# Attention scores in a two-layer decoder kernel: one fp32 product per head, or three products of high and low parts

## The chip, the cores and the metric

The kernel runs on one core of a Trainium2 chip. The metric is the device time of one execution in microseconds, lower is better. TensorE multiplies matrices into PSUM; VectorE, ScalarE and GpSimd work on tiles; SyncE issues the DMAs. Every engine takes its own instructions in the order in which they stand in its list, and waits on semaphores for the others.

## The reference

A causal decoder trunk of two layers on 512 tokens of width 1024, conditioned by a vector. Layer 0 mixes with attention, layer 1 with a state-space layer and a gated delta rule; each is followed by a convolutional feed-forward part. The change lies in layer 0's attention. It has 16 heads of 64 channels in two groups: A (8 query heads on 2 key heads, a window of 128 keys, a learned sink per head) and B (8 heads, three dilated branches). For each head:

```python
qa = rms_norm(qa.reshape(b, L, A_KV_HEADS, rep, HEAD_DIM), q_norm_a)
ka = rms_norm(ka.reshape(b, L, A_KV_HEADS, HEAD_DIM), k_norm_a)
...
s = jnp.einsum("bnqkrd,bnskd->bnkrqs", qb, kw,
               preferred_element_type=jnp.float32) * (hd ** -0.5)
...
s = jnp.where(valid[None, :, None, None], s + bias, -jnp.inf)
m = jnp.max(s, axis=-1, keepdims=True)
p = jnp.exp(s - m)
l = jnp.sum(p, axis=-1)
o = jnp.einsum("bnkrqs,bnskd->bnqkrd", p.astype(v.dtype), vw,
               preferred_element_type=jnp.float32)
```

All of it is float32.

## The kernel before, in words

**Products.** Projections, feed-forward layers and output projections are split products: each operand is held as a high part `hi` (float32 rounded to the type fp32r) and a low part `lo` (what is left), and a product is three, hi x hi, hi x lo and lo x hi, summed in one PSUM bank (`mm3`, lines 392 to 394). Attention's own products are plain fp32: scores (line 806), transposes (760 and 829) and probabilities times values (841).

**Attention** (`attention`, from line 732 on) works in chunks of 256 projected columns. Chunk 0 gives A's keys and values, chunks 1 and 2 A's queries, chunks 3 and 4 B's values, chunks 5 to 8 each one pair of B's heads, queries and keys. `project` multiplies a chunk: two groups of two token blocks, each block 24 products of 256 columns into a bank `acc`. `chunk_post` then normalises (`rmsn`) and calls `to_T`: four transposes on TensorE into bank `t` or `x`, in turn, and one pass on ScalarE (line 763) that scales them and writes an fp32 tile of 128x512, `qT` (four slots) or `kT` (two), or `kTa` for A. The two heads of a pair lie on partitions 0 to 63 and 64 to 127.

`attend` takes a pair through four blocks of 128 queries. `scores` multiplies each head's block of queries by the keys that it sees: in A 128 keys in the first block and 256 in the others, in B 128, 256, 384 and 512. Each head writes one of two banks `s`. Per head there follow on VectorE the bias and row minimum (line 819), on ScalarE the exponentials and their sum (820), on VectorE the reciprocal and the scaling (821 and 822). `values`, one block later, transposes the probabilities into the banks `t` and `x` (829), copies them to `PT` on ScalarE (832) and multiplies them by V into bank `o` (841). After its seventh step `attend` issues one row of the modulation after each block: a DMA and a reduction on VectorE (line 465). When all heads are done, their outputs are split (line 414) and the first output projection (`out_gemm`) begins, which ends attention's stage.

**Order.** A scheduler places instructions by priority and its own estimate of times; `together` keeps a list of products close behind its first one. So the order on each engine is seen in listings of the built program only. The projections of the next chunk, and at the end pieces of the output projection, fill the places between the steps of attention.

The tag of a tile names its slots: tiles of one tag share them in turn. The tags `st`, `whi` and `wlo` in attention's pool `tp` hold one 512 KB weight tile of the first chunks, its high part and its low part, one slot each, and stand empty after these.

Of the kernel before, what the change touches and what calls it, by code (L numbers as in the profile page):

```python
# [8 lines left out]
F32 = mybir.dt.float32  # L9
F32R = mybir.dt.float32r  # L10
I32 = mybir.dt.int32
AF = mybir.ActivationFunctionType
ALU = mybir.AluOpType
# [3 lines left out]
P = 128  # L17
T = 512
# [231 lines left out]
class Kernel:  # L250
# [466 lines left out]
    def attention(self):  # L717
        nc, tc = self.nc, self.tc
        I = self.I
        hA = self.open("hA", "right")  # L720
        tp = self.open("at")
        if True:
# [15 lines left out]
            def rmsn(srcs, n):  # L738

                v = tp.tile([P, 16], F32, name="qv", tag="qv", bufs=2)[:, :4 * n]  # L740
                out = []
                for b, src in enumerate(srcs):
                    qn = tp.tile([P, 2, 256], F32, name="qn", tag="qn", bufs=3)[:, :, :64 * n]
                    nc.scalar.copy(qn, src)
                    out.append(qn)
                for b, qn in enumerate(out):
                    sq = tp.tile([P, 2, 256], F32, name="qsq", tag="qsq", bufs=1)[:, :, :64 * n]
                    nc.scalar.activation(sq, qn, AF.Square)
                    nc.vector.tensor_reduce(v[:, 2 * n * b:2 * n * (b + 1)], sq.rearrange("p t (h d) -> p t h d", d=64), axis=AX.X, op=ALU.add)
                nc.vector.tensor_scalar(v, v, 1.0 / 64.0, EPS, op0=ALU.mult, op1=ALU.add)  # L750
                r = self.rsqrt(tp, v, 4 * n, f"qr{n}")
                for b, qn in enumerate(out):
                    rb = r[:, 2 * n * b:2 * n * (b + 1)].rearrange("p (t h) -> p t h", t=2).unsqueeze(3).broadcast_to([P, 2, n, 64])
                    q4 = qn.rearrange("p t (h d) -> p t h d", d=64)
                    nc.vector.tensor_tensor(q4, q4, rb, ALU.mult)
                return out

            def to_T(qns, g, gain, tag, bufs):
                pt = self.tbank()
                self.together([lambda q=q: nc.tensor.transpose(pt[:, q * P:(q + 1) * P], qns[q // 2][:, q % 2, g * P:(g + 1) * P], self.ident)  # L760
                               for q in range(4)])
                r = tp.tile([P, T], F32, name=tag, tag=tag, bufs=bufs)
                nc.scalar.activation(r, pt, AF.Copy, scale=gain)
                return r

            def chunk_post(c, accs):
                if c == 0:
                    for b in range(2):
                        nc.scalar.copy(V[:, 2 * b:2 * b + 2, 0:128], accs[b][:, :, 128:256])
                    qn = rmsn([a[:, :, 0:128] for a in accs], 2)  # L770
                    self.kTa = to_T(qn, 0, self.pcol("kga"), "kTa", 1)
                elif c in (3, 4):
                    for b in range(2):
                        o = 128 + 256 * (c - 3)
                        nc.scalar.copy(V[:, 2 * b:2 * b + 2, o:o + 256], accs[b])
                else:
                    qn = rmsn(accs, 4)
                    if c in (1, 2):
                        return [to_T(qn, g, self.qg[:, 0:1], "qT", 4) for g in range(2)]
                    return [to_T(qn, 0, self.qg[:, 1:2], "qT", 4), to_T(qn, 1, self.pcol("kgb"), "kT", 2)]  # L780

            def project(c):
                w = [self.weight(("q", c, p)) for p in range(2)]
                return chunk_post(c, [proj(c, b, w) for b in range(2)])
# [3 lines left out]
            def modulation():  # L788

                for g in (*range(16, 20), *range(8, 16)):  # L790
                    for e in range(2):
                        self.ada(0, g, (e,))
                        if e:
                            self.ada_fin(0, g, g + 1, g // 8)
                        yield

            self.step, rows = 0, modulation()

            def scores(pair, i, qT, kT, bias, isA):

                j0 = max(0, i - 1) if isA else 0
                nb = i - j0 + 1
                ps = []
                sbs = [self.bank("s")[:, :nb * P] for _ in range(2)]
                half = [slice(0, 64), slice(64, P)]
                self.together([lambda sb=sb, pr=pr: nc.tensor.matmul(sb, qT[pr, i * P:(i + 1) * P], kT[pr, j0 * P:(i + 1) * P], start=True, stop=True)  # L806
                               for sb, pr in zip(sbs, half)])
                for par, sb in enumerate(sbs):
                    bt = bias[par]
                    bt = bt[:, bt.shape[1] - nb * P:]  # L810
                    S = tp.tile([P, T], F32, name="S", tag="S", bufs=5)
                    E = S[:, :nb * P]
                    if isA:

                        E = S[:, :nb * P + 1]
                        nc.gpsimd.tensor_copy(S[:, nb * P:nb * P + 1], self.nsink[:, 2 * pair + par:2 * pair + par + 1])
                    S = S[:, :nb * P]
                    sm = tp.tile([P, 4], F32, name="sm", tag="sm", bufs=6)
                    nc.vector.tensor_tensor_reduce(S, sb, bt, -1.0, self.nsink[:, 2 * pair + par:2 * pair + par + 1] if isA else 3.0e38, op0=ALU.add, op1=ALU.min, accum_out=sm[:, 0:1])
                    nc.scalar.activation(E, E, AF.Exp, bias=sm[:, 0:1], scale=-1.0, accum_out=sm[:, 1:2])  # L820
                    nc.vector.reciprocal(sm[:, 3:4], sm[:, 1:2])
                    self.last = nc.vector.tensor_scalar(S, S, sm[:, 3:4], None, op0=ALU.mult)
                    ps.append(S)
                return pair, i, j0, nb, ps, isA
# [27 lines left out]
            def attend(pair, qT, kT, isA):  # L852
                bias = []
                for par in range(2):
                    n = 256 if isA else T
                    bt = tp.tile([P, T], F32, name="bt", tag="bt", bufs=3)[:, :n]
                    nc.sync.dma_start(bt, I["ba"][2 * pair + par] if isA else I["bb"][2 * pair + par])
                    bias.append(bt)
                for i in range(4):
                    late.append(scores(pair, i, qT, kT, bias, isA))  # L860
                    self.step += 1
                    if self.step > HELD:
                        with tc.issue_after(self.last.ins):
                            next(rows, None)
                    if len(late) > 1:
                        values(*late.pop(0))
# [57 lines left out]
            for k in range(KD):  # L924
# [9 lines left out]
                for c in range(3):  # L934
# [11 lines left out]
                    if c == 0 and k + 1 in ADA_PE:  # L946
                        next(first[k + 1])
            r = lambda a: a.rearrange("p (t n) -> p t n", t=2)
            chunk_post(0, [r(a) for a in accs[0]])
            qT = dict(zip((0, 1), chunk_post(1, [r(a) for a in accs[1]])))  # L950
            qT.update(zip((2, 3), chunk_post(2, [r(a) for a in accs[2]])))
            attend(0, qT[0], self.kTa, True)
# [4 lines left out]
            qk = project(5)  # L957
            attend(3, qT[3], self.kTa, True)
            for j in range(4):
                nxt = project(6 + j) if j < 3 else None  # L960
                attend(j, *qk, False)
                qk = nxt
# [734 lines left out]
```

## Time and profile before

| | |
|---|---|
| median of 3 runs | 1287.4 us (1284.49 to 1288.83) |
| profiled execution | 1285.57 us, span of its instructions 1283.8 us |
| TensorE busy | 1262.4 us, 98% of the span |
| VectorE busy | 1007.7 us, 78% |
| ScalarE busy | 632.2 us, 49% |
| TensorE clock granted | full in all 40 slices |

The span runs from the first to the last instruction of the profiled execution. PE stands for TensorE's products, PEld for its weight loads, DVE for VectorE, ACT for ScalarE, POOL for GpSimd. Busy times count a product until its result has left the array, so products that follow each other overlap in them. An fp32 product appears as two rows, an fp32r product as one; the profile writes f32 for both types in a product's form. In the chain of work that ended last, each piece is the time for which that work alone held the end back.

### The profile page before, as it was taken

To read this page: it belongs to the slowest core of one execution; us is meant where nothing else is said; L and a number is where in the kernel's file an instruction comes from. 1 tells how busy PE (TensorE), PEld (TensorE's weight loads), DVE (VectorE), ACT (ScalarE), POOL (GpSimd) and SP (SyncE) were. 2 spreads that over 40 slices of the span, in tenths; PEclk is the share of its full clock that TensorE was granted. 3 is DMA by queue.
4 is the path that set the end of the run, shared out by engine and by line. 5 is a ranking of instruction groups with operands and counts; after the bars stand their busy time and mean duration, and the time that the engine had idled before them with its cause. 6 is when DMAs were issued, how large, how long until landed. Compare 5 with 4: busy or idle time off the path is not lost.

```text
span 1283.8 us, 22712 instructions
## 1 busy us (share of the span) xinstructions
PE 1262.4 (98%) x8814; PEld 1079.6 (84%) x8814; DVE 1007.7 (78%) x2195; ACT 632.2 (49%) x1214; POOL 12.3 (1%) x43
## 2 busy tenths in 40 slices
PE   8999999999999999999999999999999999999998
PEld 5988775998888888778998878887999899999998
DVE  6868887679995897587678686775799999888883
ACT  4466655445532332234356555554466555555550
POOL 0001000000000000000000000000000000000000
PEclk9999999999999999999999999999999999999999
DMA  9624444615665676364444332220522223233222
GB/s 368 232 88 153 162 164 159 200 57 196 215 198 192 212 245 207 114 207 160 140 147 134 105 103 64 100 49 35 172 75 99 91 103 104 103 106 108 89 85 103
DMA packets 83133, 181.14 MB, mean 141 GB/s; under 512 B 28561, under 2 KB 36177, under 8 KB 83025
## 3 DMA queue, kind: packets, MB, share of 16 engines
q1 hardware_dynamic: 83024, 179.69, 41.5%
q8 instruction: 69, 1.13, 0.4%
q14 instruction: 40, 0.32, 0.1%
HBM read 165.55 MB, written 14.11 MB: 140 GB/s over the span
## 4 chain that ended last, share of the span: by engine, by line
PE 83%; DVE 9%; DMA 3%; ACT 3%; issue 1%; SPq 0%; DVEq 0%; ACTq 0%
PE acc L393 20%; PE acc L394 10%; PE s L393 10%; PE o L393 9%; PE s L394 5%; PE o L394 5%; PE s L626 3%; PE o L626 2%; PE acc L626 2%; PE s L806 2%; PE o L841 2%; PE x L393 1%; DVE wlo L332 1%; DMA st<-up 1%; DVE adaj L465 1%
## 5 line engine op out<-in xcount | busy, mean ns | idle before, releaser
L363 ACT CAST whi<-st 128x1024 fp32r<-128x1024 f32 (+3 forms) x168 | 165.0, 986 | 223.4 <-PE acc L393 66.3
L364 DVE TENSOR_TENSOR wlo<-st,whi 128x1024 fp32r<-128x1024 f32 (+3 forms) x168 | 191.2, 1140 | 47.2 <-ACT whi L363 45.0
L393 PE MATMUL acc<-hh,whi 128*128 128x512 f32 (+1 forms) x392 | 141.8, 367 | 2.2 <-ACT hh L550 1.8
L393 PE MATMUL acc<-hl,whi 128*128 128x512 f32 (+1 forms) x392 | 141.0, 363 | 0.2 <-DVE hl L414 0.2
L394 PE MATMUL acc<-hh,wlo 128*128 128x512 f32 (+1 forms) x392 | 140.3, 361 | 0.0
L465 DVE CUSTOM_DVE_ANT_0 adaj<-ast,cond 128x1024 bf16<-128x1024 f32 x86 | 104.8, 1219 | 7.3 <-DMA ast<-ada 7.1
L393 PE MATMUL acc<-whi,hh 128*128 128x256 f32 x320 | 93.2, 292 | 0.6 <-ACT hh L550 0.6
L394 PE MATMUL acc<-whi,hl 128*128 128x256 f32 x320 | 90.7, 283 | 0.9 <-DVE hl L551 0.9
L393 PE MATMUL acc<-wlo,hh 128*128 128x256 f32 x320 | 90.6, 284 | 0.0
L393 PE MATMUL s<-hh,whi 128*128 128x512 f32 (+2 forms) x256 | 86.8, 342 | 0.0
L393 PE MATMUL s<-hl,whi 128*128 128x512 f32 (+2 forms) x256 | 86.4, 338 | 0.0
L393 PEld LDWEIGHTS acc<-hh,whi 128*128 128x128 f32 x392 | 73.0, 188 | 15.1 <-ACT hh L550 2.4
L394 PE MATMUL s<-hh,wlo 128*128 128x512 f32 (+2 forms) x256 | 84.6, 338 | 0.0
L393 PEld LDWEIGHTS acc<-hl,whi 128*128 128x128 f32 x392 | 73.4, 188 | 12.1 <-DVE hl L414 1.0
L394 PEld LDWEIGHTS acc<-hh,wlo 128*128 128x128 f32 x392 | 73.4, 188 | 10.8
L331 ACT CAST whi<-st 128x1024 fp32r<-128x1024 f32 x54 | 56.3, 1049 | 28.0 <-DVE st L340 7.8
L393 PE MATMUL o<-hh,whi 128*128 128x512 f32 (+1 forms) x192 | 68.8, 358 | 0.0
L332 DVE TENSOR_TENSOR wlo<-st,whi 128x1024 fp32r<-128x1024 f32 x54 | 65.6, 1217 | 3.8 <-ACT whi L331 3.7
L393 PE MATMUL o<-hl,whi 128*128 128x512 f32 (+1 forms) x192 | 68.6, 357 | 0.0
L394 PE MATMUL o<-hh,wlo 128*128 128x512 f32 (+1 forms) x192 | 68.4, 356 | 0.0
L393 PEld LDWEIGHTS acc<-whi,hh 128*128 128x128 f32 x320 | 60.3, 189 | 6.1 <-issue 4.0
L393 PEld LDWEIGHTS acc<-wlo,hh 128*128 128x128 f32 x320 | 60.5, 189 | 1.6 <-issue 1.6
(909 smaller groups left out, 3468.3 us busy)
## 6 DMA issues: line engine op xcount, KB each, us to landing
ast<-ada SPq DMA_DIRECT2D x92, 512.0 KB
st<-up SPq DMA_DIRECT2D x88, 512.0 KB
st<-ri SPq DMA_DIRECT2D x20, 512.0 KB
st<-wq SPq DMA_DIRECT2D x17, 512.0 KB
st<-dn SPq DMA_DIRECT2D x16, 448.0 KB
st<-dn SPq DMA_DIRECT2D x16, 384.0 KB
st<-dn SPq DMA_DIRECT2D x16, 320.0 KB
st<-wo SPq DMA_DIRECT2D x8, 512.0 KB
```

The costliest lines, as they stand in the source:

```text
L331: nc.scalar.copy(hi, src)
L332: nc.vector.tensor_tensor(lo, src, hi.bitcast(F32), ALU.subtract)
L363: nc.scalar.copy(hi, st)
L364: nc.vector.tensor_tensor(lo, st, hi.bitcast(F32), ALU.subtract)
L393: return [lambda: mm(out, lh, rh, start=start, stop=False), lambda: mm(out, lh, rl, start=False, stop=False), lambda: mm(out, ll, rh, star ...
L394: lambda: mm(out, ll, rh, start=False, stop=stop)]
L465: self.nc.vector.tensor_tensor_reduce(junk, st, self.cond, 1.0, 0.0, op0=ALU.mult, op1=ALU.add, accum_out=self.md[l][:, i:i + 1])
L626: nc.tensor.matmul(acc, x[:, s], y, start=start and k == n == 0, stop=k == 3 and n == 2, skip_group_check=not start)
L806: self.together([lambda sb=sb, pr=pr: nc.tensor.matmul(sb, qT[pr, i * P:(i + 1) * P], kT[pr, j0 * P:(i + 1) * P], start=True, stop=True) f ...
L841: calls.append(lambda j=j, par=par, vc=vc: nc.tensor.matmul(ob[64 * par:64 * par + 64, i * P:(i + 1) * P], V[:, j0 + j, vc:vc + 64], pts[: ...
```

## The change

Queries and keys are split as well. `to_T` still transposes on TensorE; ScalarE now writes the high part, and a new instruction on VectorE computes the low part from the same bank. Both lie in one tile `qk` of 128x2x512 in fp32r. A query tile takes in turn the slots of `st`, `whi`, `wlo` and `qT`; the key tiles, A's too, share the two slots of `kT`. `scores` issues six products per block: hi x hi, hi x lo and lo x hi, each for the one head and then for the other, summed in the two banks `s`. The product lo x lo is left out.

```diff
-            def to_T(qns, g, gain, tag, bufs):
+            def to_T(qns, g, gain, tag):
+
                 pt = self.tbank()
                 self.together([lambda q=q: nc.tensor.transpose(pt[:, q * P:(q + 1) * P], qns[q // 2][:, q % 2, g * P:(g + 1) * P], self.ident)
                                for q in range(4)])
-                r = tp.tile([P, T], F32, name=tag, tag=tag, bufs=bufs)
-                nc.scalar.activation(r, pt, AF.Copy, scale=gain)
-                return r
+                if tag == "qT":
+
+                    tag = ("st", "whi", "wlo", "qT")[self.qturn % 4]
+                    self.qturn += 1
+                t = tp.tile([P, 2, T], F32R, name="qk", tag=tag, bufs=2 if tag == "kT" else 1)
+                hi, lo = t[:, 0], t[:, 1]
+                nc.scalar.activation(hi, pt, AF.Copy, scale=gain)
+                nc.vector.scalar_tensor_tensor(lo, pt, gain, hi.bitcast(F32), ALU.mult, ALU.subtract)
+                return hi, lo
...
-                    self.kTa = to_T(qn, 0, self.pcol("kga"), "kTa", 1)
+                    self.kTa = to_T(qn, 0, self.pcol("kga"), "kT")
...
-                self.together([lambda sb=sb, pr=pr: nc.tensor.matmul(sb, qT[pr, i * P:(i + 1) * P], kT[pr, j0 * P:(i + 1) * P], start=True, stop=True)
-                               for sb, pr in zip(sbs, half)])
+
+                self.together([lambda sb=sb, pr=pr, n=n, a=a, b=b: nc.tensor.matmul(
+                    sb, qT[a][pr, i * P:(i + 1) * P], kT[b][pr, j0 * P:(i + 1) * P], start=n == 0, stop=n == 2)
+                               for n, (a, b) in enumerate(((0, 0), (0, 1), (1, 0))) for sb, pr in zip(sbs, half)])
```

The calls of `to_T` lose their last argument, and `self.qturn` starts at 0.

The scheduler places the stage anew. TensorE, around the transposes of chunk 7's queries and keys (L760 before, L761 now); L806 and L814 are score products, L829 and L838 transposes of probabilities, L393 and L394 products of the projection. Before:

```order
L760 MATMUL t_2138<-ident_71,qn_2112 128x128 x2
L760 MATMUL t_2138<-ident_71,qn_2114 128x128 x2
L760 MATMUL x_2145<-ident_71,qn_2112 128x128 x2
L760 MATMUL x_2145<-ident_71,qn_2114 128x128 x2
L806 MATMUL s_2231<-kT_1857,qT_1850 128x384
L829 MATMUL t_2179<-ident_71,S_1968 128x128 x4
L829 MATMUL x_2180<-ident_71,S_1974 128x128 x4
L393 MATMUL acc_2364<-whi_2003,hh0_163 128x256
```

The change, at the same place:

```order
L761 MATMUL t_2227<-ident_71,qn_2201 128x128 x2
L761 MATMUL t_2227<-ident_71,qn_2203 128x128 x2
L761 MATMUL x_2235<-ident_71,qn_2201 128x128 x2
L761 MATMUL x_2235<-ident_71,qn_2203 128x128 x2
L814 MATMUL s_2330<-qk_1929,qk_1921 128x384 x3
L393 MATMUL acc_2471<-whi_2092,hh0_163 128x256
L393 MATMUL acc_2471<-wlo_2093,hh0_163 128x256
L394 MATMUL acc_2471<-whi_2092,hl0_164 128x256
```

The 24 products of a projection block, of which the last three rows are the first, now stand ahead of the transposes of the probabilities. The score product there is one head's, three rows in line; the other head's come later in both listings.

TensorE, the last block of the last pair, 512 keys, before:

```order
L806 MATMUL s_2718<-kT_2452,qT_2445 128x512
L841 MATMUL o_2680<-PT_2705,V_126 64x128 x2
L806 MATMUL s_2719<-kT_2452,qT_2445 128x512
L841 MATMUL o_2680<-PT_2705,V_126 64x128 x2
L829 MATMUL t_2735<-ident_71,S_2687 128x128 x3
```

The change:

```order
L814 MATMUL s_2855<-qk_2560,qk_2552 128x512
L814 MATMUL s_2856<-qk_2560,qk_2552 128x512
L814 MATMUL s_2855<-qk_2560,qk_2552 128x512
L814 MATMUL s_2856<-qk_2560,qk_2552 128x512
L814 MATMUL s_2855<-qk_2560,qk_2552 128x512
L814 MATMUL s_2856<-qk_2560,qk_2552 128x512
L838 MATMUL t_2876<-ident_71,S_2824 128x128 x3
```

The two heads, apart before, alternate here. Over the whole stage there are 41 runs of score products before and 44 now.

VectorE, the low parts of chunk 8 (L770), in the change; L828, L830 and L831 are the softmax steps of lines 819, 821 and 822 before, L465 a row of the modulation:

```order
L831 TENSOR_SCALAR S_2581<-S_2581,sm_2582 128x128
L465 ISA adaj_2589,md0_75<-ast_2587,cond_72 128x1024
L465 ISA md0_75 128x1
L770 SCALAR_TENSOR_TENSOR qk_2552<-t_2547,qg_127,qk_2552 128x512
L770 SCALAR_TENSOR_TENSOR qk_2560<-x_2555,pc_70,qk_2560 128x512
L478 TENSOR_TENSOR mb0_77<-md0_75,pc_70 128x2
L830 RECIPROCAL sm_2624<-sm_2624 128x1
L828 ISA S_2629,sm_2630<-s_2616,bt_2565 128x256
```

The two low parts stand behind a modulation row and ahead of the next softmax steps.

## Rows read from the trace of the kernel before

**Rows 1.** The page: engines' busy time, and the chain that ended last by engine and line.

```profile
PE 1262.4 (98%) x8814; PEld 1079.6 (84%) x8814; DVE 1007.7 (78%) x2195; ACT 632.2 (49%) x1214; POOL 12.3 (1%) x43
...
PE 83%; DVE 9%; DMA 3%; ACT 3%; issue 1%; SPq 0%; DVEq 0%; ACTq 0%
PE acc L393 20%; PE acc L394 10%; PE s L393 10%; PE o L393 9%; PE s L394 5%; PE o L394 5%; PE s L626 3%; PE o L626 2%; PE acc L626 2%; PE s L806 2%; PE o L841 2%; PE x L393 1%; DVE wlo L332 1%; DMA st<-up 1%; DVE adaj L465 1%
```

**Rows 2.** Busy time of each engine in attention, and in its last 39 us.

```profile
core 0: us, PE busy (x) PEld busy (x) DVE busy (x) ACT busy (x) POOL busy (x), PEclk, DMA share, GB/s
77.00:220.00 143.00, 141.04 (x1024) 104.61 (x1025) 115.67 (x417) 88.74 (x242) 8.30 (x28) 1.00 0.42 142
181.00:220.00 39.00, 37.59 (x228) 22.74 (x228) 32.73 (x117) 22.78 (x63) 0.42 (x1) 1.00 0.49 157
```

**Rows 3.** The same view, score products (L806) alone: length, PE busy, PEld busy.

```profile
77.00:220.00 143.00, 33.57 (x128) 14.04 (x128) 1.00 0.42 142
```

**Rows 4.** Chain that ended last, in attention: start us, us, what; the score products.

```profile
87.71 1.20 PE s L806 x4
...
93.02 0.42 PE s L806 x4
...
94.83 0.63 PE s L806 x4
...
96.52 0.74 PE s L806 x4
...
144.15 0.96 PE s L806 x4
...
149.60 0.84 PE s L806 x2
...
178.67 1.67 PE s L806 x4
...
198.96 1.05 PE s L806 x2
```

**Rows 5.** TensorE's timeline: start us, us, engine, line, operation; split products of the projections.

```profile
74.24 0.28 PE L393 MATMUL acc<-wlo,hh 128*128 128x256 f32 x1
74.36 0.28 PE L394 MATMUL acc<-whi,hl 128*128 128x256 f32 x1
74.48 0.28 PE L393 MATMUL acc<-whi,hh 128*128 128x256 f32 x1
74.59 0.28 PE L393 MATMUL acc<-wlo,hh 128*128 128x256 f32 x1
...
190.99 0.39 PE L393 MATMUL acc<-hh,whi 128*128 128x512 f32 x1
191.21 0.39 PE L393 MATMUL acc<-hl,whi 128*128 128x512 f32 x1
191.44 0.40 PE L394 MATMUL acc<-hh,wlo 128*128 128x512 f32 x1
```

**Rows 6.** The timeline of all engines: loads and products of two score steps.

```profile
77.04 0.30 PEld L806 LDWEIGHTS s<-kTa,qT 64*128 64x128 f32 x4
77.04 0.49 PE L806 MATMUL s<-kTa,qT 64*128 64x128 f32 x4
...
198.89 0.29 PEld L806 LDWEIGHTS s<-kT,qT 64*128 64x128 f32 x2
198.89 1.12 PE L806 MATMUL s<-kT,qT 64*128 64x512 f32 x2
```

**Rows 7.** Timeline, groups by form and waits: ScalarE's pass, VectorE's operation on PSUM, a wait.

```profile
195.50 0.69 ACT L763 ACTIVATE qT<-t,qg 128x512 f32<-128x512 f32 x1 [1.93 <-PE t L760]
...
L499 DVE SCALAR_TENSOR_TENSOR x<-acc,mb,x 128x512 f32<-128x512 f32 x20 | 14.6, 746 | 19.0 <-PE acc L394 19.0
...
PEld t L829 <- ACT qT L763: 2.5, 5, 0.8
```

**Rows 8.** Waits of VectorE in attention: in total us, times, longest us.

```profile
DVE S L819 <- PE t L829: 10.4, 7, 2.5
...
DVE S L819 <- PE s L806: 7.9, 9, 2.3
```

More of the change, by code (lines that the diff above doesn't have):

```diff
@@ L778, in chunk_post @@
                     if c in (1, 2):
-                        return [to_T(qn, g, self.qg[:, 0:1], "qT", 4) for g in range(2)]
-                    return [to_T(qn, 0, self.qg[:, 1:2], "qT", 4), to_T(qn, 1, self.pcol("kgb"), "kT", 2)]
+                        return [to_T(qn, g, self.qg[:, 0:1], "qT") for g in range(2)]
+                    return [to_T(qn, 0, self.qg[:, 1:2], "qT"), to_T(qn, 1, self.pcol("kgb"), "kT")]
             def project(c):
@@ L795, in modulation @@
                         yield
-            self.step, rows = 0, modulation()
+            self.step, rows, self.qturn = 0, modulation(), 0
             def scores(pair, i, qT, kT, bias, isA):
```

## The prediction

> **What bounds the kernel now.** I read the page first, then stretches of the trace. TensorE is busy for 98% of the span, and the chain that ended last lies on it for 83%; the products that the change touches, PE s L806, hold 2% of the span [rows 1]. So time can be won only where TensorE gives some up, and lost wherever something new makes it wait.
>
> The listings of both kernels say where to look. Up to the first score product TensorE's instructions stand as before, and from the end of the first output projection on every engine's list is the same again; only attention, about 77 to 220 us, can differ. The view of two stretches [rows 2] shows TensorE busy for 141.0 of these 143 us, VectorE for 115.7, ScalarE for 88.7. The last 39 us, after the last full projection, are tighter: VectorE has 32.7 of 39. The clock column reads 1.00, so the clock is no part of this. Score products alone fill 33.57 us of TensorE [rows 3].
>
> What does one score step occupy now? The chain gives it, waits included [rows 4]. A run of scores with both heads side by side holds TensorE 0.42 us at 128 keys and 0.63 at 256; a run of one head alone takes 0.84 at 384 and 1.05 at 512. Each 128 keys adds 0.21, and 0.21 is left as a fixed part (first weight load, drain). One head alone takes as long as two side by side, because the halves of the array run at once: at 77.04 four products of 128 columns, two per head, end within 0.49 us [rows 6]. (An fp32 product stands in the trace as two rows, each two sweeps over its columns.) Side by side is had only when both heads' score banks are free together; otherwise the second head comes later, as the 1.20 and 1.67 us runs show [rows 4].
>
> **TensorE's part.** The change puts three one-sweep products in place of one fp32 product of four sweeps. A one-sweep product starts every 0.117 us at 256 columns (74.24, 74.36, 74.48, 74.59) and every 0.225 at 512 (190.99, 191.21, 191.44) [rows 5]; half way between, 0.17 at 384. At 128 columns no such product is in the trace. Its sweep would be half of 0.117, but each product brings a weight load, and four loads on two halves fill 0.30 us, 0.19 of which is one load: a half starts its second load some 0.1 after its first [rows 6]. So I take 0.117 there too; the far bound is four sweeps as for fp32, 0.21. With the fixed 0.21, a run after the change costs 0.21 + 3 x step: 0.56 at 128 keys (was 0.42), 0.56 at 256 (0.63), 0.72 at 384 (0.84), 0.89 at 512 (1.05).
>
> Now the count of runs, by the listings.
> - Before. Group A: 4 runs of 128, 1.68; of 256, eight at 0.63, one of 1.20, one of 0.74 and two steps split into 2 x 0.63, 9.50. Group B: 128 keys, one at 0.42 and three in two halves, 2.94; 256, 3 x 0.63 and one of 0.96 (one head 0.34 behind the other), 2.85; 384, three split and one together, 5.88; 512, two of 1.67 and two split, 7.54. Together 30.4 us, near the 33.57 of [rows 3], which also counts each product's way out of the array.
> - After. A: 4 x 0.56 = 2.24; nine alternating and three split steps of 256, 15 x 0.56 = 8.40. B: 128, two alternating, one split, one with the heads one behind the other (0.79), 3.03; 256, 5 x 0.56 = 2.80; 384, three split and one heads in line (1.06), 5.38; 512, one alternating, one in line (1.34), two split, 5.79. Together 27.6.
> So TensorE is relieved of **2.7 us**: 3.4 from blocks of 256 keys and more, of which those of 128 give 0.7 back.
>
> **VectorE's part.** Each of the 13 transposed q or k tiles gets one new instruction on VectorE that reads PSUM and writes the low part. The nearest row has the same operation with a PSUM operand on 128x512: 746 ns [rows 7]; 13 x 0.746 = 9.7 us. ScalarE still makes one pass per tile (0.69 us [rows 7]), now the high part. VectorE has 27 us idle in the 143 [rows 2], 10.4 + 7.9 of them in waits for TensorE before a softmax [rows 8], so the sum fits: 125.4 of 143. Nine of the 13 come while projections still fill TensorE (24 products of 0.117, 2.8 us, between one wait and the next), and I cost them at nothing; without that cover each is 0.75. The two of chunk 7 and the two of chunk 8 come late. Those of chunk 8 have little projection work behind them: the next transposes need the banks that the low parts still read, and the softmax of the next block stands behind them in VectorE's queue. Two of 0.75 there are 1.5 us; the modulation row ahead of them (1.22 us) runs while they would wait for ScalarE anyway. Bounds: nothing (TensorE is fed with pieces of the output projection, 21 more of which now stand inside attention), and 1.5. I take **1.0**.
>
> **What moves.** In chunks 5 to 7, 24 projection products now stand between the transposes of q, k and the transposes of the probabilities; before, the latter followed at once and waited for ScalarE to empty the bank, 2.5 us over five places [rows 7]. These products are taken from other places where they covered waits, so I count no gain, with 2.5 as the bound. No DMA, bank or weight is added; the q tiles turn through four slots as before, and the k tiles through two.
>
> **Sum.** -2.7 + 1.0 = -1.7 us. The profiled execution took 1285.57 us, 1.8 around its span of 1283.8; it would become 1283.9. The median of the runs shown, 1287.4, lies 1.8 above it: **1285.7**. 0.3%, 3.9 us, is about what a measurement of this kernel can tell from no change.
>
> **The rivals.**
> - *VectorE becomes the pace of chunks 5 to 8.* It is 81% busy over the stretch and 84% in the last 39 us [rows 2]; it takes its queue in order, and each low part waits for ScalarE. From the point where TensorE waits for a softmax in every block, the eight new instructions of these chunks lie on the path and TensorE's saving turns into waiting: 8 x 0.75 = +6.0, **1293.4**. For it: VectorE's waits would be swallowed first. Against it: TensorE waits on VectorE hardly at all now. 0.17.
> - *The heads do not run side by side as one-sweep products.* Then the 19 alternating runs (6 of 128, 12 of 256, 1 of 512) have three products more: 18 x 0.35 + 0.68 = 7.0, net +5.3, **1292.7**. Against it: fp32 heads do [rows 6]. 0.05.
> - *A head's loads are not hidden under its own products.* Second and third load of each run at 256 keys and more would cost 0.107 each: 35 runs x 0.214 = 7.5, net +5.8, **1293.2**. Against it: for the 512-key step at 198.89 both loads are over within 0.29 us, under the first row's 0.43 of columns, and projections on the full array keep 0.117 a product with a new load each [rows 5, 6]. The Trainium skill, "TensorE: Matmul & The Clock Gate", in its part on packing small matmuls, says that a weight load overlaps matmuls under way only when the row group differs; by that, three products of one head would pay so, but the trace does not agree. 0.03.
> - *128-column blocks take four sweeps per product.* 6 x 0.29 for the alternating ones, 0.6 and 0.4 for the others: +2.7, net +1.0, **1288.4**. Nothing in the trace excludes it. 0.08.
> - *The better order pays too.* ScalarE's emptying of the banks is hidden and the low parts as well: -2.7 - 2.5 = -5.2, **1282.2**. For it: the listing has those 24 products in the gap. 0.22.
> - My forecast, -4 to +1 about 1285.7: 0.45.
>
> **Chances and range.** Faster by over 0.3%: 0.22 and a tail of the forecast, 0.26. Within 0.3%: the rest of the forecast and the 128-column case, 0.49. Slower: 0.17 + 0.05 + 0.03 = 0.25. The range runs from 1281.0, beyond the better order, to 1293.0, which takes in heads not side by side and leaves out the two cases above it, 0.20 together. The likeliest case alone gives 1283.4 to 1288.4.
>
> **What would show it.** Score products as three rows per head and block, in alternating runs of both heads a few ns apart, 0.56 us at 256 keys; TensorE's busy time on them near 31 us in place of 33.57; 13 instructions of 0.75 us for the low parts; VectorE near 125 us over attention; the first output projection starting within 3 us of where it did. Wrong, if TensorE waits for softmax rows on VectorE by several us more, if alternating runs at 256 take 0.9, or if a run at 128 takes over 0.8.

## The result and the profile after

The changed kernel took 1294.62 us, the median of four executions (1293.25 to 1297.54), beside 1286.47 us for the kernel before: a ratio of 1.0064, with a 95% interval of 1.0051 to 1.0078. It is **slower by about 8 us**. The forecast was 1285.7 us, and 1294.62 lies above its range of 1281.0 to 1293.0.

The page of the profiled execution (1297.54 us, span 1295.7 us) shows nothing new among the busy times: TensorE holds 98% as before [rows 1], VectorE 78%. One digit in the clock row is what matters.

```profile
PE 1271.2 (98%) x8878; PEld 1091.1 (84%) x8878; DVE 1016.4 (78%) x2208; ACT 632.4 (49%) x1214; POOL 11.3 (1%) x43
...
PEclk9999996999999999999999999999999999999999
...
PE 79%; DVE 11%; DMA 4%; ACT 4%; issue 2%; SPq 0%; DVEq 0%; ACTq 0%
```

The seventh slice (194 to 227 us) has a 6. The view of busy times by stretches, for the stretch of [rows 2] and for pieces of it, finds the place.

```profile
core 0: us, PE busy (x) PEld busy (x) DVE busy (x) ACT busy (x) POOL busy (x), PEclk, DMA share, GB/s
77.00:220.00 143.00, 140.18 (x1038) 111.17 (x1039) 115.17 (x403) 82.84 (x225) 6.83 (x27) 0.93 0.41 138
...
181.00:194.00 13.00, 13.00 (x98) 9.44 (x95) 12.22 (x47) 6.53 (x19) 0.00 (x0) 1.00 0.61 216
194.00:197.00 3.00, 1.68 (x11) 0.87 (x9) 3.00 (x10) 1.81 (x6) 0.00 (x0) 0.97 0.33 100
197.00:217.00 20.00, 19.97 (x71) 11.70 (x73) 10.14 (x37) 7.71 (x23) 0.00 (x0) 0.50 0.31 105
```

From 197 to 217 us TensorE runs at 0.50, the lower of its two levels (1.2 GHz in place of 2.4); before and behind that it has full clock. "Busy" hides it: 19.97 of 20 us. Just ahead stands a stretch in which TensorE is busy for 1.68 of 3 us. The timeline of all engines shows what it waits for (start us, us, engine, line, operation, in brackets the idle time before it and what ended it):

```profile
193.46 0.69 ACT L769 ACTIVATE qk<-t,qg 128x512 fp32r<-128x512 f32 x1 [1.12 <-PE t L761]
...
193.57 0.79 PE L814 MATMUL s<-qk 64*128 64x384 f32 x3
193.71 1.21 DVE L465 CUSTOM_DVE_ANT_0 adaj<-ast,cond 128x1024 bf16<-128x1024 f32 x1
...
194.85 0.74 DVE L770 SCALAR_TENSOR_TENSOR qk<-t,qg,qk 128x512 fp32r<-128x512 f32 x1
...
195.51 0.73 DVE L770 SCALAR_TENSOR_TENSOR qk<-x,pc,qk 128x512 fp32r<-128x512 f32 x1
...
195.65 0.66 PE L838 MATMUL t<-ident,S 128*128 128x128 f32 x4 [1.29 <-DVE qk L770]
```

This is chunk 8. ScalarE has the high part of the query at 194.15. VectorE's low part (L770) could start then, but in VectorE's queue a modulation row (L465) of 1.21 us stands ahead of it, so it starts at 194.85. The transposes of the probabilities (L838) need the bank that the low part reads, and TensorE stands idle for 1.29 us. In the kernel before, it waited there 0.56 us, for ScalarE:

```profile
196.25 0.66 PE L829 MATMUL t<-ident,S 128*128 128x128 f32 x4 [0.56 <-ACT qT L763]
```

Up to this place the change had won time: chunk 8's transposes start at 192.47, in the kernel before at 194.52, although here attention began 0.9 us later (its first transposes start at 65.02, against 64.09). The first row-sum product behind attention (L520) is a mark that both timelines have, first before, then in the changed kernel:

```profile
249.17 0.50 PE L520 MATMUL x<-ones,stat 128*128 128x1 f32 x4
...
257.32 0.61 PE L520 MATMUL x<-ones,stat 128*128 128x1 f32 x4 [0.75 <-DVE stat L507]
```

It comes 8.15 us later, as much as the medians differ. The two profiled executions lie 12.0 us apart; the rest of that comes behind this place. In what follows this start is called the stage's end.

### The profile page after: what moved, and what is told of

The parts are those of the page before. It is cut to its first block, busy times and chain, and to the rows that moved or that the text cites. A ratio compares the mean times of both kernels' runs of the same rounds, so it can differ in the third digit from the quotient of the medians.

```text
span 1295.7 us, 22847 instructions
## 1 busy us (share of the span) xinstructions
PE 1271.2 (98%) x8878; PEld 1091.1 (84%) x8878; DVE 1016.4 (78%) x2208; ACT 632.4 (49%) x1214; POOL 11.3 (1%) x43
## 4 chain that ended last, share of the span: by engine, by line
PE 79%; DVE 11%; DMA 4%; ACT 4%; issue 2%; SPq 0%; DVEq 0%; ACTq 0%
PE acc L393 18%; PE s L393 9%; PE acc L394 9%; PE o L393 9%; PE s L394 5%; PE o L394 4%; PE s L626 3%; DMA st<-up 3%; PE o L626 2%; PE acc L626 2%; PE s L814 2%; PE o L850 2%; DVE wlo L364 2%; PE x L393 1%; PE t L626 1%
## 5 line engine op out<-in xcount | busy, mean ns | idle before, releaser
L393 PE MATMUL acc<-hh,whi 128*128 128x512 f32 (+1 forms) x392 | 141.8, 367 | 2.3 <-ACT hh L550 2.3
L393 PE MATMUL acc<-hl,whi 128*128 128x512 f32 (+1 forms) x392 | 141.8, 365 | 1.1 <-DVE hl L551 0.9
L394 PE MATMUL acc<-hh,wlo 128*128 128x512 f32 (+1 forms) x392 | 140.9, 362 | 0.0
L465 DVE CUSTOM_DVE_ANT_0 adaj<-ast,cond 128x1024 bf16<-128x1024 f32 x86 | 104.8, 1219 | 7.5 <-DMA ast<-ada 7.2
L393 PE MATMUL acc<-whi,hh 128*128 128x256 f32 x320 | 93.0, 291 | 0.6 <-ACT hh L550 0.6
L394 PE MATMUL acc<-whi,hl 128*128 128x256 f32 x320 | 90.9, 284 | 0.8 <-DVE hl L551 0.8
L393 PE MATMUL acc<-wlo,hh 128*128 128x256 f32 x320 | 90.4, 283 | 0.0
L393 PE MATMUL s<-hh,whi 128*128 128x512 f32 (+2 forms) x256 | 86.8, 342 | 0.0
L393 PE MATMUL s<-hl,whi 128*128 128x512 f32 (+2 forms) x256 | 86.5, 338 | 0.0
L393 PEld LDWEIGHTS acc<-hh,whi 128*128 128x128 f32 x392 | 73.1, 189 | 14.6 <-ACT hh L550 2.9
L394 PE MATMUL s<-hh,wlo 128*128 128x512 f32 (+2 forms) x256 | 84.6, 338 | 0.0
L393 PEld LDWEIGHTS acc<-hl,whi 128*128 128x128 f32 x392 | 73.5, 189 | 13.0 <-DVE hl L551 1.1
L394 PEld LDWEIGHTS acc<-hh,wlo 128*128 128x128 f32 x392 | 73.6, 189 | 11.0 <-issue 0.2
L393 PE MATMUL o<-hh,whi 128*128 128x512 f32 (+1 forms) x192 | 68.8, 358 | 0.0
L393 PE MATMUL o<-hl,whi 128*128 128x512 f32 (+1 forms) x192 | 68.6, 357 | 0.0
L394 PE MATMUL o<-hh,wlo 128*128 128x512 f32 (+1 forms) x192 | 68.4, 356 | 0.0
L393 PEld LDWEIGHTS acc<-whi,hh 128*128 128x128 f32 x320 | 60.2, 188 | 4.0 <-ACT hh L550 1.4
L394 PEld LDWEIGHTS acc<-whi,hl 128*128 128x128 f32 x320 | 60.3, 188 | 2.5 <-DVE hl L551 1.4
```

Source lines behind the costliest of these rows:

```text
L393: return [lambda: mm(out, lh, rh, start=start, stop=False), lambda: mm(out, lh, rl, start=False, stop=False), lambda: mm(out, ll, rh, star ...
L394: lambda: mm(out, ll, rh, start=False, stop=stop)]
L465: self.nc.vector.tensor_tensor_reduce(junk, st, self.cond, 1.0, 0.0, op0=ALU.mult, op1=ALU.add, accum_out=self.md[l][:, i:i + 1])
```

## The experiments

Three theories were on the table. **A:** TensorE's idle 1.3 us at chunk 8 brings its clock down for about 20 us, and that is the loss. **B:** the one-sweep score products bring the clock down by themselves. **C:** VectorE's 13 new instructions set the pace, as the first rival of the prediction had it. Ratios are to runs of the kernel before on the same chip. The mean granted clock is given for each execution's whole span: 0.992 of 1295 us is some 21 us at 0.50 (twice 0.008 of the span), 0.996 some 10 us.

**1. Modulation rows held back.** The rows of steps 25 and 26, which stood among chunk 8's work, and all rows behind them come two steps later; nothing else is edited.

```
-                    if self.step > HELD:
+                    if self.step > HELD and self.step not in (25, 26):
```

> The change, with the modulation rows of attention's steps 25 and 26 issued two steps later, so that no 1.22 us row stands ahead of chunk 8's low parts in VectorE's queue. Theory A (TensorE waits 1.3 us for the low part behind that row, its clock falls to half for about 21 us after this gap, and that is the loss): the gap shrinks below 0.7 us, the clock stays full, 1284 to 1287. Rival B (the one-sweep products themselves lower the clock): clock low again, about 1293 to 1295. Rival C (VectorE's 13 new instructions are the pace and the clock only accompanies it): 1292 to 1294, 1.2 won.

Measured: 1286.22 us, ratio 0.9985 (0.9976 to 0.9995). The mean clock is 0.999 or 1.000 in each of ten executions, and the wait at that place has halved:

```profile
194.11 0.66 PE L838 MATMUL t<-ident,S 128*128 128x128 f32 x4 [0.63 <-DVE qk L770]
```

All 13 low parts and all products of one sweep are still there, so C falls as the cause of the loss, and B in its simple form. The stage ends at 244.44, 4.7 us ahead of the kernel before.

**2. Two products of 512 columns to fill the gap.**

```
...
+                    fill = self.bank("acc")
+                    calls += [lambda: nc.tensor.matmul(fill, self.ident, self.x[0], start=True, stop=True)] * 2
...
```

> The change, with two fp32 products of 512 columns on data of no use, into a free accumulator bank, right behind chunk 8's transposes, so that TensorE works 1.7 us where it waited 1.3. VectorE's queue keeps its row ahead of the low parts. Theory A: the clock stays full, 1285 to 1288. Rival B: clock low, 1294 to 1296. Rival C: VectorE is as late as before, 1293 to 1296.

Measured: 1295.35 us, ratio 1.0062 (1.0045 to 1.0079), clock 0.995 or 0.996 in all four. This is no clean test: the filler holds one of the two "acc" banks, and the order of all engines moved. The stretch at 0.50 came earlier, from 187 to 200 us, behind another idle place of 0.94 us (at 185.64, for ScalarE's copy), and within it TensorE also waited 1.25 and 3.36 us for VectorE. It shows only that the lower clock is not tied to the wait at chunk 8's low parts.

**3. No low part.** The low part is the high part itself. This leaves the correction out: the scores are three times hi x hi.

```
-                nc.vector.scalar_tensor_tensor(lo, pt, gain, hi.bitcast(F32), ALU.mult, ALU.subtract)
+                lo = hi
```

> The change without the low parts: no new instruction on VectorE, and all three products take the high parts, so that the scores lack their correction. TensorE's part alone. Theory A: no wait for a low part, clock full, TensorE relieved of 2.7 us: 1283 to 1286. Rival B: the clock falls as after the change, 1292 to 1295. Rival C: 1283 to 1286.

Measured: 1290.6 us, ratio 1.0016 (1.0006 to 1.0026), full clock in attention, and 0.56 us idle at that place. The stage ends at 248.77. So with 13 instructions fewer on VectorE the kernel has full clock, as A wants. A and C also expected 1283 to 1286 us; that it is no faster than the kernel before is not explained by A, B or C.

**4. fp32 products, low parts kept.** The 13 low parts are computed and not used; tile `qk` is fp32, and each head has one fp32 product again. Of the edit the products are shown.

```
-                               for n, (a, b) in enumerate(((0, 0), (0, 1), (1, 0))) for sb, pr in zip(sbs, half)])
+                               for n, (a, b) in enumerate(((0, 0),)) for sb, pr in zip(sbs, half)])
```

> The 13 new instructions on VectorE with one fp32 product per head as before; their result is not used. VectorE's part alone; in the listing no modulation row stands ahead of chunk 8's two. Theory A: the transposes wait at most 0.75 us for them, as long as before for ScalarE, clock full, 1287 to 1289. Rival B: clock full, 1287 to 1289. Rival C: slower by 5 or more, 1292 to 1296.

Measured: 1289.19 us, ratio 1.0011 (1.0000 to 1.0022). By this the 13 instructions cost about 1.2 us (1288.01 without them; the interval holds 0 to 2.8), against the 1.0 that the prediction took. I had expected a wait of at most 0.75 us. TensorE waits for the low part as long as in the changed kernel, here with no modulation row ahead of it, but also with no score product between chunk 8's transposes and the wait, and the clock stays up (0.998 in one execution, 0.999 or 1.000 in nine):

```profile
197.85 0.66 PE L838 MATMUL t<-ident,S 128*128 128x128 f32 x4 [1.35 <-DVE qk L770]
```

So A is not complete: a wait of this length does not bring the clock down whatever TensorE does around it.

**5 and 6. The wait put back in another way.** To experiment 1 the low parts of chunk 8 are added a second time, and a second and third time, so that they hold the banks longer with no modulation row near them. Shown is the first of the two edits; the other has 3 in place of 2.

```
-                nc.vector.scalar_tensor_tensor(lo, pt, gain, hi.bitcast(F32), ALU.mult, ALU.subtract)
+                for _ in range(2 if self.qturn == 8 else 1):
+                    nc.vector.scalar_tensor_tensor(lo, pt, gain, hi.bitcast(F32), ALU.mult, ALU.subtract)
```

> The kernel with the rows of steps 25 and 26 held (1286.2 us, full clock), and chunk 8's two low parts each computed twice, one pair after the other (two more instructions of 0.74 us on VectorE, behind the first pair). They keep the transposes' banks about 1.5 us longer, so TensorE's wait at that place should grow from 0.63 us to about 2. If the wait there is what brings the clock down, the granted clock falls to half behind it for some 20 us and the kernel takes about 1294 to 1296 us. If it was rather the order that the modulation row made, or its place, the clock stays full and the time is 1286.2 plus the longer wait, 1287 to 1288 us.

> As the run before, with chunk 8's low parts computed three times: the wait of TensorE should be about 3.5 us. The wait as the cause: half clock behind it, about 1296 to 1298 us. The row's order as the cause: full clock, 1288.5 to 1290 us.

Measured: twice, 1291.84 us, ratio 1.0028 (1.0018 to 1.0037); thrice, 1297.13 us, ratio 1.0063 (1.0048 to 1.0078). The waits were 2.04 and 3.36 us. Thrice has clock 0.992 in three of four executions and 0.996 in the profiled one. The view by stretches of that one:

```profile
194.00:199.00 5.00, 1.64 (x10) 1.19 (x9) 4.61 (x11) 1.75 (x4) 0.00 (x0) 0.91 0.01 2
199.00:209.00 10.00, 10.00 (x47) 6.92 (x45) 6.14 (x23) 6.03 (x17) 0.00 (x0) 0.53 0.09 29
```

Twice lies between the two theories' numbers: the clock is 0.995 to 0.997 in nine of ten executions. The profiled one is the tenth: 0.999, full clock over attention. So the longer wait comes with the lower clock without the modulation row, but not in every execution, and this wait of 2.04 us costs less clock than the changed kernel's of 1.29. Nor does the time follow the clock here: the execution at 0.999 took 1291.12 us, the nine others 1289.51 to 1295.00.

**7 and 8. Chunk 8 alone undone, chunk 8 alone changed.** In 7 the query and key of chunk 8 stay fp32 (no low part, one fp32 product per head); in 8 (`< 8` in place of `== 8`) those of all other chunks do. `scores` then issues one product per head; that part of the edit is left out here.

```
+                if self.qturn == 8:
+                    t = tp.tile([P, 2, T], F32, name="qk", tag=tag, bufs=2 if tag == "kT" else 1)
+                    nc.scalar.activation(t[:, 0], pt, AF.Copy, scale=gain)
+                    return t[:, 0], None
```

> The changed kernel with chunk 8 alone as before: its query and key stay fp32, its low parts are not computed, its scores are one fp32 product per head. 11 of 13 low parts and 24 of 32 steps' three products remain, and the modulation rows stand where they stood. If the loss hangs on TensorE's wait for chunk 8's low parts, the clock stays full and the time is about 1285 to 1288 us. If the one-sweep products of the chunks before it bring the clock down by themselves, or VectorE's work does, half clock shows around 190 to 215 us all the same and the time stays over 1292 us.

> The opposite: chunk 8 alone has high and low parts and three products, all chunks before it are as in the kernel before; the modulation row does not stand ahead of chunk 8's low parts here. The wait for the low parts alone, as the kernel with the row held had it (0.6 us): full clock, 1286 to 1289 us. If eight steps of one-sweep products behind a short wait are enough, the clock falls near 197 us and the time is 1291 to 1296 us.

Measured: 7, 1286.81 us, ratio 0.9983 (0.9974 to 0.9993), clock 0.999 or 1.000 in all ten; no idle place on TensorE over 0.5 us between 180 and 225. With 11 of 13 low parts and 28 of 32 steps in one-sweep products left (chunk 8 has four steps; the 24 in the expectation is a slip of counting), the loss is gone: it hangs on chunk 8. Experiment 8: 1289.02 us, ratio 1.0004 (0.9988 to 1.0020). I had expected a wait of 0.6 us; it was 1.35. The clock is 0.998 or more in eight of ten executions and 0.995 and 0.996 in two (1292.59 and 1294.10 us).

**9. The wait kept, TensorE given work.** Five fp32 products of 128 columns behind chunk 8's transposes, into columns of an output bank that are overwritten later. VectorE's and ScalarE's lists are those of the changed kernel, and TensorE's is longer by these five and nothing else.

```
...
+                if tag == "kT" and self.qturn == 8:
+                    fill = obs[max(obs)][:, 3 * P:]
+                    calls += [lambda: nc.tensor.matmul(fill, self.ident, self.x[0][:, 0:P], start=True, stop=True)] * 5
...
```

> The changed kernel with five fp32 products of 128 columns, whose output is overwritten later, behind chunk 8's query and key transposes: TensorE has about 1.1 us more to do before it comes to the wait for VectorE's low part. VectorE's and ScalarE's lists are word for word the changed kernel's, the modulation row stands where it stood, TensorE's list is longer by these five alone. If the loss is the idle 1.3 us in TensorE's row (the clock falls behind it), the idle time at that place shrinks to 0.3 us or less, the clock stays full and the time is 1285 to 1288 us, some 8 below the changed kernel, although there is more work and the low part comes no earlier. If the low part's lateness costs by itself, through what waits for it, or the clock falls for another reason, the time stays at 1293 to 1298 us.

Measured: 1288.14 us, ratio 0.9989 (0.9977 to 1.0001), clock 0.999 or 1.000 in all ten executions. TensorE's timeline there (the new lines move L814 to L818, L838 to L842, L770 to L774; the five products are the ten records of L765):

```profile
192.79 1.28 PE L765 MATMUL o<-x,ident 128*128 128x128 f32 x10
194.00 0.80 PE L818 MATMUL s<-qk 64*128 64x384 f32 x3
194.96 0.66 PE L842 MATMUL t<-ident,S 128*128 128x128 f32 x4 [0.17 <-DVE qk L774]
```

Counted from chunk 8's first transpose the waiting transposes start no earlier than in the changed kernel (191.79 to 194.96, 3.17 us; there 192.47 to 195.65, 3.18). The low part is as late as it was. TensorE has useless work in place of 1.1 us of idleness, and the kernel is some 10 us faster by the two ratios (0.9989 against 1.0064). So the lateness of the low part is not the loss; what TensorE does meanwhile is. Whether the shorter idle time keeps the clock up, or the fp32 products in it, this run does not tell apart. On the chip of experiments 9 to 11 the changed kernel itself was not run.

**10. The bank emptied by ScalarE.** For chunk 8, ScalarE copies the transposes to fp32 and casts the high part from the copy; VectorE subtracts from the copy, so the bank does not wait for VectorE.

```
...
+                    nc.scalar.activation(r, pt, AF.Copy, scale=gain)
+                    nc.scalar.copy(hi, r)
+                    nc.vector.tensor_tensor(lo, r, hi.bitcast(F32), ALU.subtract)
...
```

> The changed kernel, but chunk 8's transposes leave their bank by one ScalarE copy into fp32; ScalarE casts the high part from it (two more instructions of about 0.7 us) and VectorE subtracts from the copy, so that the bank no longer waits for VectorE. Two modulation rows stay among VectorE's work there, though the order around them moves. If the wait of the transposes for the bank that VectorE holds is what costs: no wait over about 0.7 us near 195 us, full clock, 1285.5 to 1288.5 us. If the modulation rows among VectorE's work are what costs, with or without that wait: 1292 us or more.

Measured: 1287.92 us, ratio 0.9986 (0.9975 to 0.9996), clock 1.000 in all ten; the longest idle place near 195 us is 0.53. Two more instructions on ScalarE and the rows among VectorE's work cost nothing that shows.

**11. Experiment 1 again, as the version to keep.**

> The kernel with the rows of steps 25 and 26 held, a second time and in more rounds, as the version to keep: ratio to the kernel before 0.998 to 0.9995, full clock in nearly every execution. If its first result was chance, the ratio's interval holds 1.

Measured: 1287.04 us, ratio 0.9981 (0.9971 to 0.9991), clock 1.000 in all twelve. Over both series the kernel with held rows is about 2 us faster than the kernel before, less than the 0.3% that the prediction calls measurable, but both intervals exclude 1.

**12. The changed kernel again.**

> The changed kernel once more, unaltered, to see in how many of its executions the clock falls. If the idle 1.3 us at chunk 8 is enough by itself, the mean granted clock is 0.992 to 0.995 in all or nearly all executions and the ratio to the kernel before is again 1.005 to 1.008. If it depends on how an execution happens to fall, as with chunk 8's low parts computed twice (0.995 to 0.999, from execution to execution), several executions show 0.997 or more and the median comes down to 1290 to 1292 us.

Measured: 1297.98 us, ratio 1.0076 (1.0062 to 1.0090). Six of seven executions have clock 0.991 or 0.992 and take 1297.06 to 1300.33 us; one has 1.000 and takes 1290.18. That one was profiled, and so the same program can be read with full clock:

```profile
194.00:197.00 3.00, 1.64 (x11) 1.03 (x10) 3.00 (x11) 1.82 (x5) 0.00 (x0) 1.00 0.46 123
197.00:217.00 20.00, 19.70 (x139) 13.40 (x138) 15.43 (x57) 12.50 (x39) 0.00 (x0) 1.00 0.41 128
```

```profile
195.39 0.66 PE L838 MATMUL t<-ident,S 128*128 128x128 f32 x4 [1.28 <-DVE qk L770]
196.05 0.66 PE L838 MATMUL x<-ident,S 128*128 128x128 f32 x4
196.78 0.43 PE L850 MATMUL o<-PT,V 128*64 128x128 f32 x2
197.14 0.79 PE L814 MATMUL s<-qk 64*128 64x384 f32 x3
197.86 0.33 PE L838 MATMUL t<-ident,S 128*128 128x128 f32 x1
```

The wait is there to within a hundredth (1.28), and the clock is not lost. In the 20 us behind it TensorE gets through 139 instructions, at 0.50 through 71; one head's three products of 384 keys take 0.79 us, at 0.50 they take 1.32. The stage ends at 248.96 in place of 257.32; from attention's start (64.55 and 65.02) that is 184.4 us in place of 192.3. So **the half clock is worth 7.9 us of the stage** within one kernel and one order of instructions, and 7.8 us lie between this execution and the median of the seven. Without it the changed kernel's stage ends 0.2 us ahead of the kernel before. The whole execution, 1290.18 us, is not faster: the kernel before took 1288.46 on that chip, 1287.32 to 1291.50.

What stays open is the condition. In experiments 1, 3, 7, 9, 10 and 11, whose profiles have no idle place of TensorE over 0.63 us around chunk 8, the mean clock is 0.999 or 1.000 in all 62 executions. The same wait of some 1.3 us came with the lower clock (0.996 or less) in 10 of the changed kernel's 11 executions, in two of ten with one-sweep products in chunk 8 alone, and in none of ten with fp32 products. That is an observed order, not a cause: these kernels also differ in what stands around the wait, and two waits of 2.04 and 1.29 us rank the wrong way round. It was not tried further.

## Why the prediction was wrong

- **The step that failed** is the sentence on [rows 2]: "The clock column reads 1.00, so the clock is no part of this." The column tells of the kernel before. The change made TensorE's wait at chunk 8 longer by 0.73 us, and the row behind it reads 0.50 for 20 us, which cost 7.9 us. No rival had this mechanism: both VectorE's part and the rival on its pace priced a wait at its own length.
- **VectorE's part** was sized about right and one reason in it was wrong. The prediction says that the modulation row ahead of chunk 8's low parts "runs while they would wait for ScalarE anyway": only in part. ScalarE was done at 194.15 and the row at 194.92, so 0.7 of its 1.21 us lay bare, and TensorE's wait grew from 0.56 to 1.29 us, by 0.73. With the 1.0 taken for it, this is no miss in length. The low parts measure 0.735 to 0.751 us each; all 13 cost about 1.2 us (experiment 4, within 0 to 2.8). VectorE's busy time from 77 to 220 us was forecast near 125; at full clock (experiment 12) it is 120.68, and three of the 13 low parts lie ahead of 77 us. At half clock it shows 115.17, no more than before [rows 2], with less of the stage in the stretch.
- **TensorE's part was right.** The three products of both heads alternate, and a run at 256 keys holds TensorE from 191.91 to 192.47, the 0.56 us of the forecast; at 128 keys it is 0.48 (below), less than the 0.56 taken, and far from the four-sweep case. One head at 384 keys takes 0.72 from start to next start (197.14 to 197.86, above), the 0.72 of the forecast.

```profile
190.54 0.55 PE L814 MATMUL s<-qk 64*128 64x128 f32 x6
191.02 0.49 PE L393 MATMUL acc<-hh,whi 128*128 128x512 f32 x1
...
191.91 0.62 PE L814 MATMUL s<-qk 64*128 64x256 f32 x6
192.47 0.32 PE L761 MATMUL t<-ident,qn 128*128 128x128 f32 x1
```

- The sum over the stage, in the view of [rows 3] for the score products alone (experiment 12's execution at full clock), went from 33.57 to 30.65 us: 2.9 saved, 2.7 forecast. The changed kernel's own profile shows 33.33, because a part of these products ran at 0.50.

```profile
77.00:230.00 153.00, 30.65 (x192) 19.41 (x192) 1.00 0.45 144
```

- The three rivals about the array itself (heads not side by side, loads not hidden, four sweeps) are out by these rows. The Trainium skill, "TensorE: Matmul & The Clock Gate", in its part on packing small matmuls, says in one place that a weight load overlaps matmuls under way only when the row group differs, and in another lets a load into the background weight buffer go ahead as well; the first alone does not agree with one head's run of 0.72 us, three loads on one row group.
- **Where the 2.9 us went** when the clock was full: the stage ended only 0.2 us earlier. 0.7 is the longer wait at chunk 8, 0.5 the later start of attention (64.55 against 64.09), and 1.1 the products with the values (23.3 us against 22.2, each record counted to the next instruction's start); why these take longer, and the last 0.4, stay open. In the order of experiments 1 and 11 the stage ends at 244.44 and 244.91, 4.7 and 4.3 us ahead of the kernel before, near the 5.2 of the rival "the better order pays too", though through rows moved on VectorE, which that rival did not have.
- Of these some 4.5 us about 2 are left at the end, and a part is lost right behind the stage. The next row-sum product (L520) starts at 265.64 in the kernel before, at 262.22 and 263.20 in experiments 1 and 11, and at 266.73 in the changed kernel with full clock: leads of 3.4 and 2.4, and a lag of 1.1 us. So with full clock, too, the changed kernel does not show the forecast gain of 1.7 us. There ScalarE comes to a weight tile of the feed-forward part before its DMA has landed, so the split of the normalised outputs behind it is late, and TensorE waits 0.86 us for that. In the kernel before, TensorE does not wait there. Experiment 1, ScalarE and TensorE:

```profile
252.56 1.05 ACT L363 CAST whi<-st 128x1024 fp32r<-128x1024 f32 x1 [3.20 <-DMA st<-up]
...
255.32 0.39 PE L393 MATMUL acc<-hl,whi 128*128 128x256 f32 x1 [0.86 <-DVE hl L551]
```

- **The rival on VectorE's pace** has 1293.4 us, near the measured time, by chance: it put the loss into waits for the softmax, while the wait that mattered is the one for the banks that the low parts read, which stands in VectorE's part. Experiment 1 keeps every one of its instructions and is faster than the kernel before.

## What to carry to other kernels

A clock column at 1.00 tells of the present order, not of the next one: where a change adds a wait at a place at which TensorE has nothing else, look for the granted clock behind it before anything else. Give the lower clock a chance of its own in the forecast, with its price: here a wait of 1.29 us was followed by a loss of some 8 us in most executions, while a wait of 1.35 us in experiment 4 cost no clock. When an operation on another engine becomes what frees a PSUM bank, look at what stands ahead of it in that engine's queue; here moving two rows that nobody was waiting for, and those behind them, turned a loss of 0.6 to 0.8% into a gain of 0.15 to 0.2%. And to test whether a late operand itself costs, or the idleness that it leaves, give the waiting engine useless work and leave the operand late.

## What the runs showed that was not expected

- TensorE's clock fell to 0.50 behind a wait of 1.29 us and stayed there for 20.5 us (196.82 to 217.30 in the profiled execution), although TensorE's row is full over that time.
- One and the same program takes either path: 1290.18 us with full clock, 1297.06 to 1300.33 without, on one chip. The kernel before shows a lower mean clock too, rarely: 1295.38 us at 0.993 and 1295.05 at 0.993, two of the 90 executions beside these experiments; where in them the clock fell, no profile shows.
- Five fp32 products that compute nothing made the changed kernel some 10 us faster.
